# One core, a hybrid retention/RG-LRU step: raw tokens transposed first and modulated two blocks ahead, gate products moved among heads, output projection by token tiles

## The chip, the core and the metric

The kernel runs on one core of a Trainium2 chip. The metric is device time in microseconds; lower is better. Five engines work in order, each from its own queue: PE (TensorE, matmul), DVE (VectorE), ACT (ScalarE), POOL (GpSimd) and SP (SyncE, which here issues nearly all DMAs). An instruction that waits holds up everything behind it on its engine.

## The reference, cut to what matters

There are 640 tokens (512 latent, 128 context), width 1024. Both groups go through the same layer.

```
mod = silu(cond) @ w_ada + b_ada ; shift, scale, gate = split(mod, 3)
h   = rmsnorm(x, norm_w) * (1 + scale) + shift           # 640 x 1024
z   = h @ w_in     # q, k, v, g_ret, x_lru, g_lru, m_ret, m_lru
o   = retention(q, k, v), 4 heads, forward + backward    # per head normalised, * silu(g_ret)
hl  = rglru(conv(x_lru)): two sigmoid gates per direction from 10 blocks of 128x128, then a scan
merged = sigmoid(m_ret) * (o @ w_ret_down) + sigmoid(m_lru) * ((hl * silu(g_lru)) @ w_lru_down)
y   = rmsnorm(x + gate * (merged @ w_out), final_norm_w) ; also the last retention and LRU states
```

## The kernel before, in words

Every fp32 product is made from three fp32r matmuls: each operand is split into a high part (ACT copies it, `hTh`, `sh`, `yh`) and a low part (DVE subtracts, `low`, line 410: `hTl`, `sl`, `yl`). Lines 404 to 406 (`mm3`) issue the three. Weights stream through SBUF: `raw` tiles are loaded by SP in a fixed stream order, split by ACT and DVE into slabs, and used by PE. Projections run feature-major with 2 x 320 tokens, so most matmuls are 128x320; those of the heads and of the output are 128x512.

The stages, in the order of PE:

1. Start. The five token tiles `x` are normalised (`norm_x`). Then for each of 8 blocks `kt` of 128 features: `mod_mm` multiplies `c` with the block's `w_ada` (tile `adr`, eight fp32 matmuls that the trace shows as 16 rows); `mod_cols` turns the result into scale and shift columns `mA`, `mB`; `x_T` transposes the five token tiles of the block into PSUM and ACT copies them to `hf`; `h_mod` applies `mA`, `mB` on DVE, ACT writes `hTh`, DVE writes `hTl`; `z_first` multiplies the block with the first three column blocks of `w_in` (18 matmuls). `mod_mm`, the transposes and `z_first` of one block are interleaved with those of the block two ahead. PSUM tiles `b1` and `b2` hold the modulation and the transposes of all blocks. Matmuls of the identity (`warm`, line 727) keep PE busy until data are there. `token_sums` prepares four sums of token halves, for the products of stage 2 (seven products in place of eight, after Strassen and Winograd).
2. 32 pairs of column blocks of `w_in` (`Pair`), each 84 matmuls of 128x320 in three parts, `one`, `two`, `three`; a pair's weights are summed by DVE (`ta`, `tb`) and split (lines 514 to 539). Results go to DRAM. Between the pairs, and later between parts of the heads, stand the gate products of the ten LRU blocks (`gates`, 24 matmuls and eight sigmoids of 128x320, line 1126); the table `GATES_AT` says where. Behind each runs a `chain` of tanh, exp, sqrt on ACT, each with a table load, and products and scans on DVE.
3. Four heads: `v_product`, `inter`, `scores`, `kv_state`, `attend`; during the next head's `v_product` the last head's output is normalised, transposed back and gated (`y_unit`, line 1481) and stored; `y_job` loads and splits it again (`yf`, `yh`, `yl`).
4. Down projection of the retention branch (`rd`, 8 blocks of 128 output columns, each in two halves `k < 8` and `k >= 8` of 48 matmuls), then that of the LRU branch (`ld`), then the output projection (`wo`) with residual and last norm (`finish_part`, `finish_end`).

PE's order is the order of the code. The order on ACT and DVE within a stage is set when the program is built: pieces of work are generators with a priority, and a planner (`Plan`, with an assumed cost for each operation) chooses which goes next on which engine (`pump`). SP's order follows from that too.

Of the kernel before, what the change touches and what calls it, by code (L numbers as in the profile page):

```python
# [14 lines left out]
D = 1024  # L15
# [28 lines left out]
def first_col(b):  # L44
# [6 lines left out]
GATES_AT = {("A", 14): 0, ("A", 20): 1, ("A", 26): 2, (0, "kv"): 3, (1, "sc"): 4, (1, "at"): 5,  # L51
            (2, "at"): 6, (3, "at"): 7, (4, 0): 8, (4, 4): 9}


def stream_order():
    def gates(h, at):
        return [("gt", GATES_AT[h, at])] if (h, at) in GATES_AT else []

    o = [("fm", NEXT)]
    for n in range(len(PAIRS)):  # L60
        o += [("pa", n), ("pb", n)] + gates("A", n - 1)

# [205 lines left out]
class Direct:  # L268
# [20 lines left out]
P_X, P_C = 1.5, 1.5  # L289
# [3 lines left out]
def tile_hybrid_step(  # L293
# [188 lines left out]
    def split(i, raw, when, pools, keep=False):  # L482
# [6 lines left out]
        else:  # L489
            yield If(turn(i, pools, when))  # L490
            hi, lo = slab.take(pools() if reg[0] is not None else (perm,))
# [9 lines left out]
    def pair_weights(i, r0, r1, when):  # L501
# [20 lines left out]
        def part(sub, k):  # L522
            yield If(turn(i - 1, lambda: (perm, reg[0]), when, sub))
            hi, lo = slab.take((perm, reg[0]))
# [27 lines left out]
    def gate_sum(i, m, src, when):  # L552
        yield If(lambda: when if m == 0 or f"w{i - 3}" in S.named and S.named[f"w{i - 3}"].done else None)
# [160 lines left out]
    b1 = psp.tile([128, 512], F32, tag="b0", name="b")  # L714
    b2 = psp.tile([128, 512], F32, tag="b1", name="b")
# [24 lines left out]
    def mod_mm(kt):  # L740
        for k in range(8):
            g = slice(32 * (k % 4), 32 * (k % 4) + 32)
            w = ada_raw[kt][k // 2][:, 256 * (k % 2):256 * (k % 2) + 256]
            pe.matmul(out=b2[g, 0:256], lhsT=c32[:, k], rhs=w, start=(k < 4), stop=(k > 3))  # L744
        S.pe += 900.0
        for t in ada_raw.pop(kt):
            ada.give(t)
        dve0.tensor_copy(mod4[kt % 2], b2[:, 0:256])

    def mod_cols(kt):  # L750
        m = mod4[kt % 2]
        sel = pv[:, V_SEL:V_SEL + 2]
        pe.matmul(out=b2[:, 256:258], lhsT=m[:, 0:128], rhs=sel, start=True, stop=True)
        pe.matmul(out=b2[:, 258:260], lhsT=m[:, 128:256], rhs=sel, start=True, stop=True)
        S.pe += 250.0
        dve0.tensor_scalar(mB[:, kt], b2[:, 256:258], col(V_BSH, kt), None, op0=ADD)
        dve0.tensor_scalar(mA[:, kt], b2[:, 258:260], bsc1[:, kt:kt + 1], col(V_NW, kt), op0=ADD, op1=MUL)

    fulls, ready = {}, {}

    def x_T(kt):
        full = wide("hf")
        fulls[kt] = full
        for t in (4, 0, 1, 2, 3):
            o = b2[:, 384:512] if t == 4 else b1[:, 128 * t:128 * t + 128]
            pe.transpose(o, xt[t][:, 128 * kt:128 * kt + 128], ident)
        S.pe += 600.0
        act0.activation(full[:, 512:640], b2[:, 384:512], AF.Copy)
        act0.activation(full[:, 0:512], b1, AF.Copy)
# [7 lines left out]
    def h_low(kt):  # L777
        dve0.tensor_tensor(hTl[:, kt], fulls[kt], f32(hTh[:, kt]), op=SUB)
# [10 lines left out]
    def token_sums(k):  # L789
        a1, a2 = fulls[k], fulls[k + 4]  # L790
        a11, a21, a12, a22 = a1[:, 0:H], a1[:, H:NT], a2[:, 0:H], a2[:, H:NT]
        yield If(W6.room(2))
        u, w = wide("su"), wide("sw")
        s1, s2, s3, s4_ = u[:, 0:H], u[:, H:NT], w[:, 0:H], w[:, H:NT]
        yield V(H)
        dve.tensor_tensor(s1, a21, a22, op=ADD)
        yield V(H)
        dve.tensor_tensor(s2, s1, a11, op=SUB)
        yield A(NT)
        act.activation(sTh[0][:, k], u, AF.Copy)  # L800
# [12 lines left out]
        low(sTl[1][:, k], w, sTh[1][:, k])
        W6.give(w)

    def modulate(kt):
        mod_cols(kt)
        h_mod(kt)
        h_low(kt)

    for t in range(5):
        norm_x(t)
        warm(6)
    wf_high(0)
    wf_low(0)
    x_T(0)
    warm(4)
    mod_mm(0)
    load_ada(4)
    load_wf(4)  # L830
    warm(4)
    modulate(0)
    x_T(1)
    wf_high(1)
    wf_low(1)
    mod_mm(1)
    modulate(1)
    zq = [psz(), psz(), psz()]
    prep = soft()
    S.pe = 23000.0  # L840
    for e in S.clock:
        S.clock[e] = 23000.0

    def z_first(i, kt):
        S.pe = max(S.pe, ready[kt])
        fm_k([zq[i][:, 0], zq[i][:, 1]], wf_hl[kt], 128 * i, hTh[:, kt], hTl[:, kt], kt == 0, kt == 7)
        if kt > 3:
            S.pump(S.pe - 500.0)

    for kt in range(8):  # L850
        z_first(0, kt)
        if kt < 6:
            x_T(kt + 2)
            wf_high(kt + 2)
        z_first(1, kt)
        if kt < 6:
            mod_mm(kt + 2)
            wf_low(kt + 2)
        z_first(2, kt)
        if kt < 6:  # L860
            modulate(kt + 2)
# [7 lines left out]
        if kt == 3:  # L869
            job(prep, "soft", prio=4.0)  # L870
        if kt > 1 and kt < 6:
            job(token_sums(kt - 2), f"sums{kt - 2}", prio=1.5)
# [20 lines left out]
    zs = [b1, b2]  # L893
# [16 lines left out]
    for n in ["first0", "first1", "first2", "soft"] + [f"sums{k}" for k in range(4)]:  # L910
# [17 lines left out]
    tts.add(rg, [f"tt{i}" for i in range(3)])  # L928
    tmps = Slots(S)
    tmps.add(rg, ["p0", "p1"])  # L930
# [271 lines left out]
    WL.add(rg, [f"l{i}" for i in range(8)])  # L1202
    lru_jobs(("A",))
    prev = None
    for n in range(len(PAIRS) + 1):
        p = None
        if n < len(PAIRS):
            p = Pair(n)
            p.one()
        if prev:  # L1210
            prev.three()
            hook("A", n - 1)
        if p:
            p.two()
        prev = p

# [7 lines left out]
    def switch_to_heads():  # L1224
        S.until(lambda: not (W6.busy(rg) or WL.busy(rg) or tmps.busy(rg) or tts.busy(rg) or slab.busy(rg) or half.busy(rg)))
        for s in (W6, WL, tmps, tts, slab, half):
            s.drop(rg)
        reg[0] = None
        regp.__exit__(None, None, None)
        sTp.__exit__(None, None, None)  # L1230
# [50 lines left out]
    def v_product(h, between):  # L1281
        acc = {}
        for kk in range(4):
# [13 lines left out]
            between(kk)  # L1297
# [35 lines left out]
    def prompt_k(h):  # L1333
# [23 lines left out]
        job(ev(), f"kd{h}", prio=2.0)  # L1357
# [159 lines left out]
    def fetch_qk(h):  # L1517
        for s in "qk":
            for i in range(2):
                job(qk_job(s, h, i), f"{s}{h}{i}", prio=1.6)  # L1520

    for h in range(NH):
        def between(kk, h=h):
            if h == 0 and kk == 0:
                switch_to_heads()
# [417 lines left out]
```

## Time and profile before

| | |
|---|---|
| median of 3 runs | 1025.45 us (1022.33 to 1027.98) |
| the profiled execution | 1029.65 us, span from first to last instruction 1027.8 us |
| PE busy | 993.9 us (97% of the span) |
| DVE, ACT busy | 738.1 us (72%), 529.8 us (52%) |
| mean granted PE clock | 0.98 |
| DMA | 158.15 MB, mean 154 GB/s |

Busy is the time in which an engine had an instruction in work; matmuls overlap, so PE's share says only that PE rarely had none. The granted clock is the share of 2.4 GHz that PE was given; 0.50 is 1.2 GHz.

### The profile page before, as it was taken

What the parts mean: (1) busy time and instruction counts of PE and PEld (TensorE: products, weight loads), DVE (VectorE), ACT (ScalarE), POOL (GpSimd) and SP (SyncE); (2) the same over time, 40 slices, a digit from 0 to 9 for tenths busy, and PEclk for the clock granted to TensorE, in tenths of its full rate; (3) what the DMA queues carried; (4) which work ended last, traced back from release to release, by engine and by line L of the source; (5) the groups of instructions that cost most, each with busy time, mean ns of one, the idle gap of its engine ahead of it and who ended that gap; (6) DMA issues with size and microseconds to landing.
All of it is one profiled execution on the core that took longest, in us unless ns stands there. A gap on an engine that the chain in (4) does not pass through costs nothing.

```text
span 1027.8 us, 15490 instructions
## 1 busy us (share of the span) xinstructions
PE 993.9 (97%) x6057; PEld 926.3 (90%) x6057; DVE 738.1 (72%) x1148; ACT 529.8 (52%) x835; POOL 2.2 (0%) x13
## 2 busy tenths in 40 slices
PE   8987999999999999999999998999989999999996
PEld 7877999999999999999888887878869999999885
DVE  4578986777689879885576776687778974846436
ACT  5345544444675684563359277557566616424203
POOL 0000000000000000000000000000000000000000
PEclk8988999999999999999999998999999999999999
DMA  9623554443425325535433542553547655635402
GB/s 344 208 98 95 161 164 142 134 134 123 141 101 208 128 94 187 195 114 176 168 92 129 176 148 78 181 180 105 184 161 252 221 176 186 220 107 183 157 1 103
DMA packets 62168, 158.15 MB, mean 154 GB/s; under 512 B 6906, under 2 KB 10126, under 8 KB 62094
## 3 DMA queue, kind: packets, MB, share of 16 engines
q1 hardware_dynamic: 62094, 157.16, 46.4%
q8 instruction: 47, 0.77, 0.3%
q14 instruction: 27, 0.22, 0.1%
HBM read 119.51 MB, written 37.63 MB: 153 GB/s over the span
## 4 chain that ended last, share of the span: by engine, by line
PE 88%; DVE 4%; ACT 3%; DMA 3%; issue 1%; SPq 0%; ACTq 0%; DVEq 0%
PE z L404 29%; PE z L406 28%; PE z L405 28%; PE b L744 1%; DVE sl L410 1%; DMA wfr<-in_w_first_dram 1%; DMA hf<-h 1%; DMA y<-sg 1%; PE z L1481 1%; DMA yf<-y 0%; DMA x<-in_x_sample_dram 0%; ACT z L1433 0%; DVE ptl L410 0%; DVE ltl L410 0%; DVE st L1375 0%
## 5 line engine op out<-in xcount | busy, mean ns | idle before, releaser
L410 DVE TENSOR_TENSOR sl<-raw,sh 128x1024 fp32r<-128x1024 f32 (+1 forms) x128 | 133.4, 1046 | 53.5 <-ACT sh L495 52.6
L495 ACT ACTIVATE sh<-raw 128x1024 fp32r<-128x1024 f32 (+1 forms) x96 | 96.7, 1012 | 144.1 <-PE z L405 89.8
L404 PE MATMUL z<-sh,sh 128*128 128x320 f32 x512 | 159.9, 312 | 7.0 <-ACT sh L529 5.9
L406 PE MATMUL z<-sh,sl 128*128 128x320 f32 x512 | 159.8, 312 | 0.7 <-DVE sl L410 0.7
L405 PE MATMUL z<-sl,sh 128*128 128x320 f32 x512 | 159.7, 312 | 0.0
L404 PE MATMUL z<-hTh,sh 128*128 128x320 f32 x432 | 137.1, 317 | 0.0
L405 PE MATMUL z<-hTl,sh 128*128 128x320 f32 x432 | 135.1, 313 | 0.0
L406 PE MATMUL z<-hTh,sl 128*128 128x320 f32 x432 | 134.9, 312 | 0.0
L404 PEld LDWEIGHTS z<-sh,sh 128*128 128x128 f32 x512 | 97.3, 190 | 7.5 <-ACT sh L529 6.2
L406 PEld LDWEIGHTS z<-sh,sl 128*128 128x128 f32 x512 | 97.2, 190 | 1.1 <-DVE sl L410 1.1
L405 PEld LDWEIGHTS z<-sl,sh 128*128 128x128 f32 x512 | 97.3, 190 | 0.0
L404 PEld LDWEIGHTS z<-hTh,sh 128*128 128x128 f32 x432 | 82.8, 192 | 2.9 <-issue 2.5
L405 PEld LDWEIGHTS z<-hTl,sh 128*128 128x128 f32 x432 | 82.7, 191 | 0.0
L406 PEld LDWEIGHTS z<-hTh,sl 128*128 128x128 f32 x432 | 82.6, 191 | 0.0
L404 PE MATMUL z<-yh,sh 128*128 128x320 f32 x256 | 79.3, 310 | 0.0
L406 PE MATMUL z<-yh,sl 128*128 128x320 f32 x256 | 79.2, 309 | 0.0
L405 PE MATMUL z<-yl,sh 128*128 128x320 f32 x256 | 79.2, 309 | 0.0
L404 PE MATMUL z<-sh,hTh 128*128 128x512 f32 x160 | 64.3, 402 | 0.6 <-ACT gt L1126 0.6
L405 PE MATMUL z<-sl,hTh 128*128 128x512 f32 x160 | 63.5, 397 | 0.0
L406 PE MATMUL z<-sh,hTl 128*128 128x512 f32 x160 | 63.4, 396 | 0.0
L405 PE MATMUL z<-ltl,sh 128*128 128x320 f32 x160 | 49.6, 310 | 0.5 <-DVE ltl L410 0.5
L404 PE MATMUL z<-lth,sh 128*128 128x320 f32 x160 | 49.6, 310 | 0.0
(252 smaller groups left out, 2200.3 us busy)
## 6 DMA issues: line engine op xcount, KB each, us to landing
raw<-in_w_str_dram SPq DMA_DIRECT2D x131, 512.0 KB, 3.9
adr<-in_w_ada_dram SPq DMA_DIRECT2D x32, 256.0 KB, 5.2
g<-c SPq DMA_DIRECT2D x16, 320.0 KB, 2.3
sg<-g SPq DMA_DIRECT2D x16, 320.0 KB, 3.5
y<-sg SPq DMA_DIRECT2D x16, 320.0 KB, 2.6
yf<-y SPq DMA_DIRECT2D x16, 320.0 KB, 4.6
out_dram<-kv SPq DMA_DIRECT2D x16, 256.0 KB, 2.6
x<-c SPq DMA_DIRECT2D x10, 320.0 KB, 4.0
```

The source lines that it names most:

```text
L404: pe.matmul(out=out, lhsT=lh, rhs=rh, start=start, stop=False, **kw)
L405: pe.matmul(out=out, lhsT=lh, rhs=rl, start=False, stop=False, **kw)
L406: pe.matmul(out=out, lhsT=ll, rhs=rh, start=False, stop=stop, **kw)
L410: dve.tensor_tensor(out, full, f32(hi), op=SUB)
L495: act.activation(hi[:, 0:w], raw, AF.Copy)
L744: pe.matmul(out=b2[g, 0:256], lhsT=c32[:, k], rhs=w, start=(k < 4), stop=(k > 3))
L1481: pe.transpose(z[:, 128 * t:128 * t + 128] if t < 4 else zp_[:, 0:128], o[t][:, 128 * i:128 * i + 128], ident)
```

## The change

In words, in the order of the program:

- **Start.** The transposed tokens no longer wait for the modulation of their block. All eight `x_T` stand ahead of the first `z_first`, in the three large PSUM tiles `z`; blocks 1 and 3 are copied out by DVE. `mod_mm` alternates between two PSUM tiles (`mb`), `mod_mm`, `mod_cols` and `h_mod` run two blocks ahead; `h_mod` moves from DVE to ACT (Identity with scale and bias), and for blocks 0 and 1 both engines do it (ACT straight into `hTh`). There are 15 more identity matmuls ahead and 4 fewer behind. The tokens' tiles move to the other side of SBUF, so that the tiles for the pairs' weights (`ta`, `tb`, `p`) open before the first block and not behind stage 1.
- **Token sums.** Split into `sum_3` and `sum_124`, started as soon as their blocks are there, at a higher priority.
- **Gates.** Seven of ten gate products move (`GATES_AT`), four of them in heads 0 to 2, to an earlier place; the planner's costs and some priorities change.
- **Last pair.** The first quarter of head 0's `v_product` now stands ahead of the last part of the last pair.
- **Down projection.** New order of the 16 halves (`DOWN`): (0,0), (1,0), (2,0), then (0,1) and so on; head 3's four `y_unit` stand behind the first and the second of them, not ahead of all.
- **Output.** The k-outer loop over three token tiles at once is replaced by one token tile after the other.

```diff
-GATES_AT = {("A", 14): 0, ("A", 20): 1, ("A", 26): 2, (0, "kv"): 3, (1, "sc"): 4, (1, "at"): 5,
-            (2, "at"): 6, (3, "at"): 7, (4, 0): 8, (4, 4): 9}
+GATES_AT = {("A", 10): 0, ("A", 20): 1, ("A", 26): 2, (0, "sc"): 3, (1, "v3"): 4, (1, "kv"): 5,
+            (2, "sc"): 6, (3, "at"): 7, ("D", 5): 8, ("D", 9): 9}
...
+DOWN = [(0, 0), (1, 0), (2, 0), (0, 1), (1, 1), (2, 1), (3, 0), (4, 0), (3, 1), (4, 1), (5, 0), (6, 0), (5, 1), (6, 1),
+        (7, 0), (7, 1)]
...
-    def h_mod(kt):
+    def h_mod(kt, both=False):
         full = fulls[kt]
-        for c, g in ((slice(0, 512), 1), (slice(512, 640), 0)):
-            dve0.tensor_scalar(full[:, c], full[:, c], mA[:, kt, g:g + 1], mB[:, kt, g:g + 1], op0=MUL, op1=ADD)
-        act0.activation(hTh[:, kt], full, AF.Copy)
...
+            if both:
+                act0.activation(hTh[:, kt, c], full[:, c], AF.Identity, scale=a, bias=b)
...
+                act0.activation(full[:, c], full[:, c], AF.Identity, scale=a, bias=b)
+        if not both:
+            act0.activation(hTh[:, kt], full, AF.Copy)
+        dve0.tensor_tensor(hTl[:, kt], full, f32(hTh[:, kt]), op=SUB)
...
     for t in range(5):
         norm_x(t)
-        warm(6)
+        warm(9)
+    x_T(0)
+    x_T(1, dve0)
...
+    mod_mm(0, dve0)
...
+    x_T(7)
+    xtp.__exit__(None, None, None)
+    ttp, tr = open_pool("ttp", "right")
+    tts.add(tr, [f"tt{i}" for i in range(3)])
...
     for kt in range(8):
         z_first(0, kt)
+        if kt == 0:
+            mod_cols(1)
+            h_mod(1, True)
         if kt < 6:
-            x_T(kt + 2)
+            mod_mm(kt + 2)
             wf_high(kt + 2)
         z_first(1, kt)
         if kt < 6:
-            mod_mm(kt + 2)
+            mod_cols(kt + 2)
             wf_low(kt + 2)
+            h_mod(kt + 2)
         z_first(2, kt)
-        if kt < 6:
-            modulate(kt + 2)
...
+        if n == len(PAIRS):
+            next(v_first)
         if prev:
             prev.three()
...
+    for n, (m, half_k) in enumerate(DOWN):
+        if n in (1, 2):
+            for i in (2 * n - 2, 2 * n - 1):
+                y_unit(NH - 1, i)
+        if n == 2:
+            switch_to_down()
...
+    for t, c0, n, i in parts:
...
+        accs = [bank()] if t else [bank(), bank()]
+        for k in range(8):
+            if t == 0:
+                wo[k] = take(("wo", k))
+                need(f"ml{k}")
+            for b, a in enumerate(accs):
+                out_mm(a[:, 0:n], c0 + 512 * b, n, t, k)
```

Three places of the instruction order. First PE at the start, where the identity matmuls ahead of the first transposes end; before:

```order
L766 MATMUL b<-ident,x_110 128x128
L727 MATMUL z<-ident 128x128 x4
L744 MATMUL b<-adr,c_114 32x256 x8
L727 MATMUL z<-ident 128x128 x4
L753 MATMUL b<-pv,mod_112 128x2
L754 MATMUL b<-pv,mod_112 128x2
L766 MATMUL b<-ident,x_111 128x128
```

The same place now (L781 is `x_T`, L754 `mod_mm`, L766 and L767 `mod_cols`):

```order
L781 MATMUL z<-ident,x_111 128x128
L736 MATMUL b<-ident 128x128 x2
L754 MATMUL b<-adr,c_117 32x256 x8
L781 MATMUL z<-ident,x_107 128x128
L781 MATMUL z<-ident,x_108 128x128
L781 MATMUL z<-ident,x_109 128x128
L781 MATMUL z<-ident,x_110 128x128
L781 MATMUL z<-ident,x_111 128x128
L736 MATMUL b<-ident 128x128 x2
L766 MATMUL b<-pv,mod_115 128x2
L767 MATMUL b<-pv,mod_115 128x2
L781 MATMUL z<-ident,x_107 128x128
```

Block 2's transposes stand between block 0's modulation matmuls and its columns, and more transposes follow directly; before, the columns stood between two stretches of identity matmuls.

Second, ACT at the passage from the start to the first pair. Before (`m<-z`, `m<-b` are the first sigmoids, `sw`, `su` the token sums, `p<-z` the copy of pair 0's first product, `tb`, `ta` pair 0's summed weights):

```order
L886 ACTIVATE m<-z 128x640
L904 ACTIVATE m<-b 128x320 x2
L811 ACTIVATE sh_101<-sw 128x640
L800 ACTIVATE sh_100<-su 128x640
L811 ACTIVATE sh_101<-sw 128x640
L707 ACT_TABLE_LOAD
L707 ACTIVATE qdec<-qdec 128x32
L708 ACTIVATE kdec<-kdec 128x8
L952 ACTIVATE p<-z 128x320
L539 ACTIVATE sh<-raw 128x512
L495 ACTIVATE sh<-raw 128x1024
L539 ACTIVATE sh<-raw 128x512
```

Behind these follow, before, the splits of `tb` and `ta` (L529). Now:

```order
L944 ACTIVATE m<-z 128x640 x2
L848 ACTIVATE sh_100<-s_765 128x640
L944 ACTIVATE m<-z 128x640
L848 ACTIVATE sh_100<-s_803 128x640
L539 ACTIVATE sh<-tb 128x1024
L962 ACTIVATE m<-b 128x320 x2
L539 ACTIVATE sh<-ta 128x1024
L858 ACTIVATE sh_101<-s_764 128x2x320
L1007 ACTIVATE p<-z 128x320
```

The split of `tb` has moved ahead of `m<-b`, that of `ta` directly behind it, and the table load with `qdec`, `kdec` to a later place.

Third, ACT in head 1, where the gates' sigmoids stood at the end of the head (L1126 `gt`; L1433 squares of the head's output, L1440 its norm, L1158 the chain's square root, L1413 `kv`):

```order
L1158 ACTIVATE th<-th 128x640
L1427 ACTIVATE o<-z 128x512
L1433 ACTIVATE z,ssq<-o 128x512 x2
L1440 ACTIVATE rst<-ssq,epsc 128x5
L1158 ACTIVATE th<-th 128x640
L1126 ACT_TABLE_LOAD
L1126 ACTIVATE gt<-z,pv 128x320 x4
L1413 ACTIVATE kv<-z 128x512 x2
```

In head 1 now, the first of the two gate products stands behind the last quarter of `v_product` (L1317 splits `v`, L1181 is `gt`, L1361 the start of `inter`):

```order
L1317 ACTIVATE vh<-z 128x512 x5
L505 ACTIVATE sh<-raw 128x1024
L1181 ACT_TABLE_LOAD
L1181 ACTIVATE gt<-z,pv 128x320 x4
L505 ACTIVATE sh<-raw 128x512
L1181 ACTIVATE gt<-z,pv 128x320 x2
L1361 ACTIVATE o<-z,qdec 128x512
L1181 ACTIVATE gt<-z,pv 128x320 x2
```

The second gate product of head 1 moved from behind `attend` to between `kv_state` and `attend`.

## Rows read from the trace of the kernel before

**Rows 1.** The page: span and PE's line.
```profile
span 1027.8 us, 15490 instructions
...
PE 993.9 (97%) x6057; PEld 926.3 (90%) x6057; DVE 738.1 (72%) x1148; ACT 529.8 (52%) x835; POOL 2.2 (0%) x13
```

**Rows 2.** PE's waits over the span: total us, times, longest.
```profile
PE z L404 <- ACT sh L529: 5.9, 1, 5.9
PE b L744 <- ACT hf L284: 5.7, 3, 4.3
PE z L404 <- ACT gt L1126: 2.7, 2, 2.1
PE z L404 <- ACT pph L1378: 2.1, 1, 2.1
PE z L1481 <- ACT gt L1126: 1.5, 1, 1.5
```

**Rows 3.** Windows: length, busy us by engine, PE clock, DMA share, GB/s.
```profile
28.00:32.84 4.84, 4.84 (x48) 4.06 (x44) 2.93 (x7) 1.80 (x4) 0.00 (x0) 1.00 1.00 326
49.90:55.80 5.90, 1.58 (x13) 1.32 (x10) 4.61 (x10) 2.52 (x5) 0.00 (x0) 0.85 0.25 86
55.80:64.00 8.20, 8.18 (x40) 6.91 (x41) 3.59 (x8) 2.55 (x4) 0.00 (x0) 0.50 0.22 65
77.90:84.20 6.30, 0.36 (x3) 0.16 (x1) 5.31 (x17) 5.92 (x10) 0.00 (x0) 0.77 0.07 11
84.20:91.60 7.40, 6.65 (x24) 6.25 (x25) 7.33 (x10) 2.23 (x3) 0.00 (x0) 0.50 0.52 144
100.00:150.00 50.00, 50.00 (x343) 50.00 (x342) 43.29 (x62) 26.40 (x40) 0.00 (x0) 1.00 0.49 154
```

**Rows 4.** Timeline of PE: start, us, line, operation; first transposes, block 0, pair 1.
```profile
12.79 0.77 PE L766 MATMUL b<-ident,x 128*128 128x128 f32 x5 [0.38 <-DVE x L284]
13.40 1.06 PE L727 MATMUL z<-ident 128*128 128x128 f32 x8
14.71 1.07 PE L744 MATMUL b<-adr,c 128*32 128x256 f32 x16 [0.26 <-ACT hf L284]
...
22.66 0.61 PE L404 MATMUL z<-hTh,sh 128*128 128x320 f32 x1
...
93.41 0.31 PE L404 MATMUL z<-hTh,sh 128*128 128x320 f32 x1
```

**Rows 5.** Groups by shape in 0 to 60 us: count, busy us, mean ns, idle before.
```profile
L284 ACT ACTIVATE hTh<-hf 128x640 fp32r<-128x640 f32 x7 | 5.2, 738 | 23.6 <-DVE hf L284 23.6
...
L284 DVE TENSOR_TENSOR hTl<-hf,hTh 128x640 fp32r<-128x640 f32 x7 | 5.8, 825 | 5.6 <-ACT hTh L284 5.6
```

**Rows 6.** Windows in heads 1 and 3 and behind.
```profile
564.00:592.00 28.00, 28.00 (x134) 22.91 (x133) 20.93 (x33) 7.29 (x11) 0.00 (x0) 1.00 0.51 171
599.00:625.00 26.00, 23.49 (x117) 19.82 (x115) 17.64 (x28) 22.68 (x40) 0.00 (x0) 0.98 0.47 146
625.00:631.00 6.00, 5.19 (x17) 4.81 (x18) 4.54 (x7) 4.83 (x11) 0.00 (x0) 0.51 0.23 87
746.00:750.00 4.00, 1.91 (x9) 1.16 (x7) 4.00 (x8) 2.14 (x5) 0.00 (x0) 1.00 0.79 252
750.00:754.00 4.00, 4.00 (x12) 2.98 (x11) 3.74 (x6) 2.26 (x5) 0.00 (x0) 0.57 0.94 346
```

**Rows 7.** Timelines of SP and DVE at the start of the down projection.
```profile
774.81 1.86 SPq L591 DMA_DIRECT2D y<-sg  x2
776.72 3.79 SPq L596 DMA_DIRECT2D yf<-y  x8
...
790.17 0.82 DVE L410 TENSOR_TENSOR yl<-yf,yh 128x640 fp32r<-128x640 f32 x1
```

**Rows 8.** Timeline of the end: last matmul, last stores.
```profile
1019.31 0.28 PE L406 MATMUL z<-sh,ml 128*128 128x256 f32 x1
...
1023.08 1.94 SPq L1779 DMA_DIRECT2D out_dram<-u  x4
```

More of the change, by code (lines that the diff above doesn't have):

```diff
@@ L490, in split @@
             yield If(turn(i, pools, when))
-            hi, lo = slab.take(pools() if reg[0] is not None else (perm,))
+            hi, lo = slab.take([p for p in pools() if p is not None])
         grant(i)
@@ L523, in part @@
             yield If(turn(i - 1, lambda: (perm, reg[0]), when, sub))
-            hi, lo = slab.take((perm, reg[0]))
+            hi, lo = slab.take([p for p in (perm, reg[0]) if p is not None])
             grant(i - 1, sub)
@@ L759, in tile_hybrid_step, with x_T @@
+        pe.matmul(out=b[:, 258:260], lhsT=m[:, 128:256], rhs=sel, start=True, stop=True)
+        S.pe += 300.0
+        dve0.tensor_scalar(mB[:, kt], b[:, 256:258], col(V_BSH, kt), None, op0=ADD)
+        dve0.tensor_scalar(mA[:, kt], b[:, 258:260], bsc1[:, kt:kt + 1], col(V_NW, kt), op0=ADD, op1=MUL)
     fulls, ready = {}, {}
-    def x_T(kt):
+    groups = ((slice(0, 512), 1), (slice(512, 640), 0))
+    def x_T(kt, eng=act0):
         full = wide("hf")
         fulls[kt] = full
-        for t in (4, 0, 1, 2, 3):
-            o = b2[:, 384:512] if t == 4 else b1[:, 128 * t:128 * t + 128]
+        z = psz()
+        for t in range(5):
+            o = z[:, 1, 0:128] if t == 4 else z[:, 0, 128 * t:128 * t + 128]
@@ L1200, in hook @@
             gates(j)
[L1202 to L1215, printed above, removed]
     hdp = [None]
@@ L1224, in switch_to_heads @@
     def switch_to_heads():
-        S.until(lambda: not (W6.busy(rg) or WL.busy(rg) or tmps.busy(rg) or tts.busy(rg) or slab.busy(rg) or half.busy(rg)))
-        for s in (W6, WL, tmps, tts, slab, half):
+        S.until(lambda: not (W6.busy(rg) or WL.busy(rg) or tmps.busy(tr) or tts.busy(tr) or slab.busy(rg) or half.busy(rg)))
+        for s in (W6, WL, slab, half):
             s.drop(rg)
@@ L1279, in v_job, with v_product @@
         banks.give(ps)
-    def v_product(h, between):
+    def v_product(h):
         acc = {}
@@ L1519, in fetch_qk @@
             for i in range(2):
-                job(qk_job(s, h, i), f"{s}{h}{i}", prio=1.6)
-    for h in range(NH):
-        def between(kk, h=h):
-            if h == 0 and kk == 0:
-                switch_to_heads()
-                job(strip_job(0), "strip0", prio=3.0)
-                lru_jobs(range(5))
+                job(qk_job(s, h, i), f"{s}{h}{i}", prio=1.4)
+    WL.add(rg, [f"l{i}" for i in range(8)])
+    lru_jobs(("A",))
+    prev, v_first = None, v_product(0)
+    for n in range(len(PAIRS) + 1):
+        p = None
+        if n < len(PAIRS):
+            p = Pair(n)
+            p.one()
+        if n == len(PAIRS):
+            next(v_first)
+        if prev:
+            prev.three()
+            hook("A", n - 1)
+        if p:
+            p.two()
+        prev = p
+    switch_to_heads()
+    job(strip_job(0), "strip0", prio=3.0)
+    lru_jobs((0, 1, 2, 3, "D"))
+    fetch_qk(0)
+    for h in range(NH):
+        for kk in v_first if h == 0 else v_product(h):
             if h and kk:
                 y_unit(h - 1, kk - 1)
-            if h == 0 and kk == 0:
-                fetch_qk(0)
             hook(h, f"v{kk}")
-        v_product(h, between)
         if h:
@@ L1552, in tile_hybrid_step @@
         hook(h, "at")
-    for i in range(4):
-        y_unit(NH - 1, i)
-        S.pump()
-    hd = hdp[0][1]
-    S.until(lambda: not (W6.busy(hd) or W5.busy(hd)))
-    W6.drop(hd)
-    W5.drop(hd)
-    hdp[0][0].__exit__(None, None, None)
-    regC = ctx.enter_context(tc.tile_pool(name="regC", bufs=1, reuse_waits="tile"))
-    W6.add(regC, [f"c{i}" for i in range(38)])
-    for i in range(8, 16):
-        job(y_job(i // 4, i % 4, W6), f"y_{i}", prio=1.0)
     sig, ro = {}, {}
@@ L1715, in tile_hybrid_step @@
         W6.give(lt[k][1])
-    S.until(lambda: all(S.named[f"w{i}"].done for i in range(len(order)) if order[i][0] == "ga" and f"w{i}" in S.named))
+    need("ga7")
     load_rows(0, gbias)
```

286 lines of the change are left out of this document (157 added, 129 removed).

## The prediction

> **What bounds the kernel now.** I read the page first, then PE's waits, then windows over the stretches in which PE's share is low, then the timelines there. PE has something in work for 97% of the span [rows 1], so PE's order is the path that sets the end, and 33.9 us without PE work are all that its waits can hold. But a busy PE is not always a fast PE: in four stretches the granted clock is 0.50 or little more, that is 1.2 GHz [rows 3, 6], and each of them follows a wait. A steady stretch shows the full rate: 343 matmuls of 128x320 in 50 us, 0.146 us each, at clock 1.00 [rows 3].
>
> Two of the waits stand in the passage from the start to the first pair: the modulation matmuls of block 7 wait 4.3 us for ACT to empty the PSUM tile with block 7's transposes, and pair 0's second product waits 5.9 us for its split weights [rows 2]. After each, PE runs at 1.2 GHz, for 8.2 us (55.8 to 64.0) and 7.4 us (84.2 to 91.6) [rows 3]. The rest stands in the heads: 2.1 us for `gt` at the end of head 1, 2.1 us for `pph` in head 3, 1.5 us for `gt` ahead of head 3's `y_unit` [rows 2]; the first two are again followed by clock 0.51 and 0.57 over 6 and 4 us [rows 6].
>
> **The change, term by term. The front.** Before, block 0's first product starts at 22.66 and pair 1 at 93.41 [rows 4]; I count how long the new order takes to the same two points.
>
> To block 0: the identity matmuls now run 15 longer, 30 rows in the trace. Eight rows take 1.06 us [rows 4], 0.13 each; so they end some 3 to 4 us after the 12.79 at which transposes began before, near 16. Behind them PE has eight sets of transposes (0.55 to 0.77 us, upper end as in [rows 4]), two `mod_mm` at about 1.0 (1.07 there), four identity matmuls and one `mod_cols`, together about 1.0: 7.4 to 9.2 us, so 23.4 to 25.2. ACT and DVE copy out meanwhile; block 0's `hTl` needs five PSUM copies, `hTh` and DVE's own 0.83 [rows 5] behind the tokens, and comes at about 24 too. I take 24.0: a loss of 1.3 against 22.66.
>
> From there each block costs what block 28.00 to 32.84 costs, 4.84 us [rows 3], less one set of transposes (0.55 to 0.77) and a wait of some 0.1 to 0.2: 4.1. It can be no less, since 18 matmuls at 0.146 are 2.6 and the modulation takes 1.5. Can ACT keep that? Per block it has the copy of `mod`, the weights' high part, two parts of `h_mod` and `hTh` 0.74 [rows 5], under 3.3 us with a token sum, and the results are needed a block later; so PE sets the period. Six blocks of 4.1 and two of 2.6 give 29.8, the column block behind them 48 x 0.146 = 7.0, pair 0's first two products 24 x 0.146 = 3.5, its next three 36 x 0.146 = 5.3. Sum from 24.0: pair 1 at 69.6, with some 0.9 for small waits 70.5, against 93.41: **-23**.
>
> Nothing may wait then at the passage. Before, the tiles of `tb` and `ta` opened only behind stage 1, and the token sums stood ahead of them. Now the tiles are free at the start, and in ACT's order the split of `tb` stands ahead of `m<-b`. From block 7's `hTl` at about 51, DVE has about 13 us of work up to `sl<-tb`, ready at about 64 against the 64.8 at which PE wants it. That is tight: what DVE loses there, PE waits. The bounds of this term are -25 (no small waits) and -13 (the wait of 5.9 stays, with its slow stretch, in which 24 matmuls do the work of 3.5 us in 6.7).
>
> A rule bears on the clock. The Trainium skill, "TensorE: Matmul & The Clock Gate", section "HAM oscillation — how this bites in real kernels", says that waits between groups of matmuls make the clock fall and that each restart is paid anew. The trace agrees: waits of 4.3 and 5.9 us are followed by 0.50 [rows 2, 3], while the 1.5 us for `gt` cost no clock. By that rule the new front, whose waits are under 1 us, stays at 2.4 GHz; if it did not, the third rival below would hold.
>
> **The heads.** At 599 to 625 ACT is busy 22.7 of 26 us, at 564 to 592 only 7.3 of 28 [rows 6]: head 1 has two gate products behind its scores, whose 16 sigmoids, tanh, exp, sqrt and table loads all fall into the same stretch. Moving the first into `v_product` puts some 11 us of ACT work (an estimate: eight sigmoids, six passes over 640 columns, three table loads) into the slack. What is left for ACT from the scores to the norm I sum to about 21 us against 24 us of PE work. So the 3.3 us without PE work (2.5 of the 26 and 0.8 of the 6) go, and the 6 us at 0.51 lose about 2.7 us less: **-6**. Against it: DVE has 20.9 of 28 busy there already [rows 6] and gets about 10 us of the first chain, where 7.1 are free; I set **+1** for waits on late `v`, `o` and `st`, bounds 0 and +4. The wait of 1.0 at the last pair is covered by 30 matmuls of 128x512 that now stand ahead (about 6.8 us), and the shorter waits for `gt` and `hl` parts behind moved gates go as well: **-2** together, bounds 0 and -3.
>
> Head 3's wait for `pph` I leave: ACT stands behind `yh`, which waits for loads of `y`, and SP's order there is nearly the same as before; now three `yh` instead of two stand between the first and the second score tile. **0**, bounds -3.7 (2.1 and the clock) and +1.
>
> **Down projection.** The 1.5 us for `gt` is covered by the first half (0,0), 48 x 0.146 = 7.0 us. But head 3's last two `y_unit` now stand behind it and (1,0), and only (2,0), 7 us, lies between them and (0,1), which needs all of heads 2 and 3. Before, the last `yl` came at 791.0, 14.3 us after the first of the eight loads at 776.7, and 14 us of matmuls lay between [rows 7]. Now the loads can be issued some 2.6 us behind the last `y_unit`, and `yl` 8 is wanted 13.2 us behind it: 2.6 + 14.3 - 13.2 = 3.7 us late, less what DVE is spared of gate 7's chain and of gate sums. I take 2: **+0.5** net, bounds -1.5 and +2.2.
>
> **The end.** The output projection has the same matmuls. Its first tile now takes a slab of `w_out` every 1.3 us instead of 3.9, but the last operand `ml7` is wanted 9 us behind the LRU projection and takes about 6. Before, the finish of token tile 3 ran into that of tile 4: behind the last matmul (1019.31 + 0.28) four stores were issued, the last at 1025.0 [rows 8]. Now DVE and ACT have one tile there, and the last of two stores goes out some 1.7 us earlier: **-1.7**, bounds -0.5 and -2.5.
>
> **Sum.** -23 - 6 + 1 - 2 + 0 + 0.5 - 1.7 = -31.2. The profiled execution took 1029.65, so 998.5 for such a one; it stands 4.2 above the median of the runs shown (1025.45), and in medians the sum gives 994.3. I say **995 us**.
>
> **The rivals.** *Head work returns.* The front gains, but the heads' waits only change their place: DVE in head 1 is the new bound (+4), the down projection waits its 3.7, and nothing else is won. -23 - 1.7 + 4 + 2.2 - 2 = -20.5, so 1005. For it speaks DVE's 20.9 of 28 [rows 6]; against it that ACT, not DVE, was full where PE waited.
>
> *Pair 0's weights stay late.* The wait in front of the second product stays: -13 for -23 in the front, so 1005 again, or 1010 together with half of the first rival. For it speaks the margin of under 1 us; against it that DVE is not held by anything but its own order.
>
> *Slower: the front stays cold.* If the granted clock stood at 0.50 from the first transposes on, as at 55.8 to 64.0, a matmul of 128x320 would take 0.27 and not 0.146 (24 in 6.65 us at 84.2 to 91.6 [rows 3]), 1.85 times as long. The 54 us from 16 to 70 would cost 46 more: 995 + 46 = 1041. It decides from 37 us of such work on (31.2 / 0.85). Against it: from 28 us on the old kernel runs at 1.00 with the same mix [rows 3], and the new one has PE fuller.
>
> *No effect.* PE has work 97% of the time already [rows 1], so nothing is to be had but what waits hold; if the freed stretches were taken up by other waits, 1025. The Trainium skill, "Perfetto Trace Analysis", section "Identifying the Most-Contended Engine", calls PE's busy share a bad measure of what is left. The trace agrees: 40 rows took 8.2 us at 55.8 to 64.0 and count as 8.18 busy [rows 3].
>
> **Chances.** Forecast 0.58 (its own range 986 to 1001); head work returns 0.20 (1001 to 1010); late weights 0.13 (1002 to 1014); no effect 0.05; slower 0.04. 984 comes about if head 3's wait and the down projection's go too; I leave out 2 in 10, mostly above, and give 985 to 1010. A measurement of this kernel can tell about 0.5%, 5 us, from no change: faster 0.91, within 0.5% 0.05, slower 0.04.
>
> **What would show it.** Right: first product of block 0 near 24 us; blocks every 4.1 us; pair 1 near 70; no clock under 0.9 between 20 and 90; no wait for `tb` or `ta`; ACT fuller in head 1's `v_product` and no wait for `gt` at its end; a wait of some 2 us for `yl` at (0,1); two stores behind the last matmul. The forecast is wrong if pair 1 starts behind 78, or if the waits from 480 us on sum to as much as before.

## The result, and the profile after

The changed kernel takes 998.67 us (median of 4 runs, 998.22 to 999.64) against 1026.49 us before (4 runs on the same chip, 1022.33 to 1027.98): ratio 0.9737, 95% interval 0.9706 to 0.9768. The profiled execution took 999.01 us against 1029.65. The forecast was 995 (985 to 1010): the sign and the main places were right, and four steps were mis-sized or wrong.

The page after: span, busy time of the engines; to be read beside [rows 1].
```profile
span 997.2 us, 15542 instructions
...
PE 981.6 (98%) x6079; PEld 918.0 (92%) x6079; DVE 732.3 (73%) x1133; ACT 543.6 (55%) x856; POOL 2.2 (0%) x13
```
PE is busy 12 us less while the span is 31 us shorter: 18 us of waits went, and 12 us of busy time, for the most part matmuls at 1.2 GHz. PE's waits after, total, times, longest, beside [rows 2] (L414 to L416 are `mm3` now, L420 is `low`, L294 a helper through which ACT and DVE get their work at the start):
```profile
PE z L414 <- ACT pph L1419: 2.9, 1, 2.9
PE z L414 <- ACT gt L1181: 1.5, 1, 1.5
...
PE z L414 <- ACT hTh L294: 1.1, 1, 1.1
PE z L415 <- DVE yl L420: 1.0, 1, 1.0
```
PE's timeline after, to be read beside [rows 4]: the first transposes, block 0, pair 1.
```profile
15.18 1.25 PE L781 MATMUL z<-ident,x 128*128 128x128 f32 x10
...
23.11 0.41 PE L414 MATMUL z<-hTh,sh 128*128 128x320 f32 x1
...
73.92 0.31 PE L414 MATMUL z<-hTh,sh 128*128 128x320 f32 x1
```
The waits of 5.9 for `sh`, 4.3 for `hf` and 2.1 for `gt` are gone; the one for `pph` has stayed and grown.

To see where the time came from I took the first product of each stage from PE's timeline in both traces. Between pair 1 and the LRU projection the two kernels do the same PE work (head 3's four `y_unit` are in both), so the differences add up to that of the spans:

| stretch of PE's order | before, us | after, us | difference | forecast |
|---|---|---|---|---|
| start to pair 1 | 93.41 | 73.92 | -19.5 | -23 |
| pair 1 to head 1's first product | 461.63 | 459.50 | -2.1 | -2, with the rest of the heads |
| head 1 | 74.14 | 69.12 | -5.0 | -6 + 1 |
| head 2 | 68.00 | 65.10 | -2.9 | (in the -2) |
| head 3 and down projection | 193.52 | 195.20 | +1.7 | 0 + 0.5 |
| LRU and output projections | 128.89 | 128.12 | -0.8 | 0 |
| end of the last matmul to end of span | 8.25 | 6.28 | -2.0 | -1.7 |
| sum | 1027.8 | 997.2 | -30.6 | -31.2 |

Windows after (length, busy us by engine, PE clock, DMA share, GB/s): a block of the front, the stretch ahead of block 7's first product, head 1's `v_product`, head 1 from its scores on, and head 3 around its scores.
```profile
28.60:32.90 4.30, 4.30 (x40) 3.52 (x39) 2.67 (x7) 3.37 (x7) 0.00 (x0) 1.00 1.02 371
49.10:53.95 4.85, 3.73 (x26) 3.48 (x26) 3.17 (x12) 1.99 (x4) 0.00 (x0) 1.00 0.14 23
542.00:570.00 28.00, 28.00 (x141) 23.52 (x141) 22.18 (x34) 15.93 (x24) 0.00 (x0) 1.00 0.51 172
577.00:603.00 26.00, 25.95 (x124) 21.69 (x123) 23.90 (x37) 22.67 (x41) 0.00 (x0) 1.00 0.50 160
715.00:720.00 5.00, 2.80 (x13) 1.97 (x11) 5.00 (x10) 3.93 (x8) 0.00 (x0) 1.00 0.77 267
720.00:725.00 5.00, 4.35 (x13) 3.54 (x14) 4.89 (x9) 4.56 (x10) 0.00 (x0) 0.71 0.36 137
```
A block takes 4.30 us (4.84 in [rows 3]). Head 1's `v_product` has 15.9 us of ACT work where [rows 6] had 7.3; ACT is as full from the scores on as it was, but PE no longer waits there. Head 3's wait for `pph` is still followed by a low clock. The kernel before had a fifth slow stretch, which the prediction does not name: from 20 to 27 us, around its block 0, the mean clock was 0.52. It is gone too.

### The profile page after: what moved, and what is told of

Its sections match the earlier page's. It is cut to its first block, busy times and chain, and to the rows that moved or that the text cites. A ratio compares the mean times of both kernels' runs of the same rounds, so it can differ in the third digit from the quotient of the medians.

```text
span 997.2 us, 15542 instructions
## 1 busy us (share of the span) xinstructions
PE 981.6 (98%) x6079; PEld 918.0 (92%) x6079; DVE 732.3 (73%) x1133; ACT 543.6 (55%) x856; POOL 2.2 (0%) x13
## 4 chain that ended last, share of the span: by engine, by line
PE 91%; DVE 4%; ACT 3%; issue 1%; DMA 1%; POOL 0%; DVEq 0%; POOLq 0%; ACTq 0%
PE z L414 29%; PE z L415 29%; PE z L416 29%; PE b L736 1%; PE z L1522 1%; ACT hf L294 1%; DVE sl L420 1%; ACT hTh L294 1%; DVE hTl L294 1%; DMA y<-sg 0%; DMA yf<-y 0%; ACT sh L539 0%; PE z L781 0%; ACT gt L1181 0%; DVE st L1416 0%
## 5 line engine op out<-in xcount | busy, mean ns | idle before, releaser
L420 DVE TENSOR_TENSOR sl<-raw,sh 128x1024 fp32r<-128x1024 f32 (+1 forms) x128 | 133.2, 1045 | 50.2 <-ACT sh L505 49.8
L414 PE MATMUL z<-sh,sh 128*128 128x320 f32 x512 | 158.5, 310 | 0.7 <-ACT p L1007 0.7
L416 PE MATMUL z<-sh,sl 128*128 128x320 f32 x512 | 158.4, 309 | 0.0
L414 PE MATMUL z<-hTh,sh 128*128 128x320 f32 x432 | 134.6, 311 | 1.1 <-ACT hTh L294 1.1
L416 PE MATMUL z<-hTh,sl 128*128 128x320 f32 x432 | 133.2, 308 | 0.0
L414 PEld LDWEIGHTS z<-sh,sh 128*128 128x128 f32 x512 | 96.1, 188 | 1.3 <-ACT p L1007 1.3
L416 PEld LDWEIGHTS z<-sh,sl 128*128 128x128 f32 x512 | 96.1, 188 | 0.0
L414 PEld LDWEIGHTS z<-hTh,sh 128*128 128x128 f32 x432 | 81.1, 188 | 3.9 <-issue 2.5
L416 PEld LDWEIGHTS z<-hTh,sl 128*128 128x128 f32 x432 | 81.1, 188 | 0.0
L414 PE MATMUL z<-yh,sh 128*128 128x320 f32 x256 | 79.4, 310 | 1.6 <-ACT gt L1181 1.5
L416 PE MATMUL z<-yh,sl 128*128 128x320 f32 x256 | 79.0, 309 | 0.0
L414 PE MATMUL z<-sh,hTh 128*128 128x512 f32 x160 | 63.7, 398 | 0.0
L416 PE MATMUL z<-sh,hTl 128*128 128x512 f32 x160 | 63.2, 395 | 0.0
L1054 ACT ACTIVATE p<-z 128x320 f32<-128x320 f32 x32 | 14.0, 437 | 67.3 <-PE z L416 67.3
L414 PEld LDWEIGHTS z<-yh,sh 128*128 128x128 f32 x256 | 48.1, 188 | 2.2 <-ACT gt L1181 1.7
```

What stands on the lines that cost most here:

```text
L414: pe.matmul(out=out, lhsT=lh, rhs=rh, start=start, stop=False, **kw)
L416: pe.matmul(out=out, lhsT=ll, rhs=rh, start=False, stop=stop, **kw)
L420: dve.tensor_tensor(out, full, f32(hi), op=SUB)
L1054: act.activation(self.tmp[:, 2], self.a[:, 0:H], AF.Copy)
```

## The experiments

Each is an edit of the changed kernel, except the first. In all of them the computation is unchanged. They were measured on several chips, each beside the kernel before, whose medians there lay between 1025.7 and 1026.9 us. The changed kernel was not measured again, so a difference of 1 or 2 us from its 998.67 is weak by itself; the stages of the profiled executions are read with it.

**1. The front alone.** The kernel before, with the new start, block loop, token sums and place of the tiles for `ta` and `tb`, and nothing else of the change.

> The kernel before with the new front alone (start, block loop, token sums, place of the tiles for ta and tb); gates, heads, down projection and output stay as before. Theory: the terms add up, so this kernel starts pair 1 near 73.9 us, as the changed one does, and takes 19.5 us less than before, 1007 us, with head 1's wait for gt (2.1 us, clock near 0.5 behind it) still there. Rival: the front's gain leans on what was changed behind it, or the later stages take part of it back by waits for loads and splits that now come earlier: pair 1 near 74 all the same, but a time of 1012 us or more.

Measured: 1009.97 us against 1026.02, ratio 0.9842 (0.9811 to 0.9873). Pair 1 starts at 74.40, with a mean clock below 1 behind block 7, which the changed kernel's profile does not have; head 1 waits 1.2 and 2.1 us as before, and head 3 and the down projection take 193.8 us as before. The profiled execution took 1010.13, 19.5 less than the profiled one of before, as the theory has it; the medians differ by 16.0 only. The time lies between the theory's 1007 and the rival's 1012. In profiled executions the terms add up, and the mark that I set was wrong in the same way as the forecast: it took the difference of two profiled executions off a median (below).

**2. Gates back.**
```diff
-GATES_AT = {("A", 10): 0, ... (0, "sc"): 3, (1, "v3"): 4, (1, "kv"): 5, (2, "sc"): 6,
+GATES_AT = {("A", 14): 0, ... (0, "kv"): 3, (1, "sc"): 4, (1, "at"): 5, (2, "at"): 6,
```


> The changed kernel with gate products 0 to 6 at their old places (7, 8 and 9 stay at the new ones). Theory: the places of the gates are what shortened heads 1 and 2 by 5.0 and 2.9 us, since ACT was full behind head 1's scores: the time comes back to 1006 or 1007 us, with a wait of some 2 us for gt at the end of head 1 and a granted clock near 0.5 behind it. Rival: most of it came from the changed priorities (splits of q and k, kd, the gate chains) and the early first slab of head 0: then the time is 1002 us or less and head 1 has no wait over 1 us for gt.

Measured: 1004.89 us, ratio 0.9797 (0.9769 to 0.9825), 6.2 above the changed kernel's median. PE's waits for `gt` in this run, of which 2.7 us stand at the end of head 1 and 1.5 ahead of half (0,0):
```profile
PE z L414 <- ACT gt L1181: 4.2, 2, 2.7
```
Heads 1 and 2 take 72.13 and 65.67 us in place of 69.12 and 65.10. The time stays under the theory's 1006, and the clock behind the wait was 1.00 and not near 0.5. So the places of the gates are worth 5 to 6 of the 8 us that I gave them: 6.2 by the medians, and by the stages of the profiled execution 3.0 in head 1, 1.5 in the pairs and 0.6 in head 2. The other 2.3 us of head 2's gain come from elsewhere in the change. In the kernel before, head 2 has waits of 0.6 us for `kdh` and 0.6 for a slab of weights, which are gone, and the end of the slow stretch behind head 1; which edit took them away, no run here shows.

**3. Old order of the down projection**, with head 3's `y_unit` ahead.
```diff
-DOWN = [(0, 0), (1, 0), (2, 0), (0, 1), (1, 1), (2, 1), (3, 0), (4, 0), (3, 1), (4, 1), ...
+DOWN = [(0, 0), (1, 0), (0, 1), (1, 1), (2, 0), (3, 0), (2, 1), (3, 1), (4, 0), (5, 0), ...
-        if n in (1, 2):
-            for i in (2 * n - 2, 2 * n - 1):
+        if n == 0:
+            for i in range(4):
```


> The changed kernel with the down projection's halves in the old order and head 3's four y_unit ahead of them. Theory: the new order covered nothing, since half (0,0) itself waits for the PSUM banks that gate 7's sigmoids hold; undone, the wait for gt (1.5 us) moves to the first y_unit, the wait for yl (1.0 us) goes, and head 3 with the down projection takes 194 us in place of 195.2; whole time 997.5 us. Rival, as I forecast: the new order saves the 1.5 us, so undone it costs them and saves 1.0: 999.2 us or more.

Measured: 1001.58 us, ratio 0.977 (0.9743 to 0.9797). The wait of 1.5 for `gt` moved to the first `y_unit` and that for `yl` fell to 0.3, as the theory says. But two waits of 1.1 us came up that neither theory has: the gates behind the sixth and tenth half now find four PSUM banks held by half-done products. Head 3 and the down projection take 199.3 us, 5 more than forecast; the rival's time came (999.2 or more), but not by its cause. So the run does not price the order alone; it shows that the new order saved nothing on the `gt` wait, and that these two gates cost 1.1 us each where products are open and nothing in the changed kernel, where none is.

**4. Old output loop.** `finish` and the output loop as before the change.

> The changed kernel with the output projection's old loop (three token tiles at once over k, then tiles 3 and 4). Theory: the new loop gains behind the last matmul alone, 8.5 us before against 6.5 now; undone, four stores go out behind the last matmul and the time is 2.0 us higher, 1000.7 us, with the same 57.3 us from the first product to the last. Rival: the tail is set by tile 4 alone, so it stays at 6.5 us and the time within 0.5 us of 998.7.

Measured: 1000.50 us, ratio 0.9757 (0.9732 to 0.9782). The 57.6 us from the first output product to the end of the last matmul are the same; behind it stand 8.2 us in place of 6.3. The new loop is worth 2 us, all in the tail.

**5. Block 7 ahead of the sums.**
```diff
-        S.pump(S.pe)
+        if (kt, i) not in ((4, 2), (5, 0), (5, 1)):
+            S.pump(S.pe)
```


> The changed kernel with DVE's token sums of the last two blocks of the modulation put behind block 7's mB, mA and hTl instead of ahead of them; soft's eight short operations stay. Theory: the 1.1 us for hTh and 0.4 for hTl before block 7's first product are there because four sums and splits (2.2 us) stand ahead of mB in DVE's queue; without them block 7 starts 1.5 to 2 us earlier, pair 1 about 49.3 us behind block 0's first product in place of 50.8 to 51.7, and the time is 997.0 us. Rival: DVE is the bound of this stretch, since from 48 to 68 us it is idle for only 1.6 us; then the same time is lost a little later, at pair 0's S2 or S1 products, and pair 1 stays 50.5 us or more behind block 0.

Measured: 998.03 us, ratio 0.9735 (0.9696 to 0.9773). PE's waits from 20 to 80 us, of this run:
```profile
PE z L414 <- ACT p L1008: 1.5, 1, 1.5
PE z L415 <- DVE hTl L294: 0.5, 2, 0.3
```
The wait for `hTh` is gone and has come back 15 us later: pair 1 stands 50.78 us behind block 0's first product, 50.81 in the changed kernel. The rival holds: with block 7 ahead in DVE's queue, something else is late.

**6. Also `soft` later.** `soft`'s short operations run behind pair 2.

> As the run with block 7 ahead, and soft's operations (2.3 us of DVE between 49 and 66 us) moved behind pair 2. If DVE is the bound of the stretch, taking 2.3 us of its work out gains up to as much: pair 1 about 48.8 us behind block 0 and 996.5 us. If the order alone was at fault, this run is like the one before it, within 0.3 us in the front.

Measured: 997.97 us, ratio 0.9737 (0.9688 to 0.9787), pair 1 50.4 us behind block 0: 0.4 us for 1.6 us of DVE work less (the expectation says 2.3; `soft`'s eight operations sum to 1.6 in the trace). What is last there is a chain over both engines: `p`'s copy (the wait is 1.8 us now) stands on ACT behind the last sums' `sh`, which waits for DVE.

**7. Loads of `y` later.**
```diff
     def y_job(h, i, slots):
+        if h < 2 and 4 * h + i > 1:
+            yield after(f"st{NH - 1}3")
```


> The changed kernel with six of the eight loads and splits of y in head 3 held back until its fourth score tile is split. Theory: the 2.9 us for pph come from the yh that wait for their loads in ACT's queue ahead of the score tiles' splits (one of them 2.5 us); without them the wait goes, and with it the stretch at clock 0.71: head 3 up to the down projection 4 us shorter, 994.5 us. Rival: the score tiles are late because of DVE (strip product, splits, and 5 us of conv) or the splits of y now stand in front of attend's evictions: the wait only moves, and the time stays above 997.5 us.

Measured: 993.60 us, ratio 0.969 (0.9652 to 0.9728). Windows of this run around head 3's scores:
```profile
715.00:720.00 5.00, 5.00 (x24) 3.66 (x23) 5.00 (x10) 3.02 (x7) 0.00 (x0) 1.00 1.00 372
720.00:725.00 5.00, 5.00 (x24) 4.13 (x23) 4.67 (x9) 2.68 (x5) 0.00 (x0) 1.00 0.92 312
```
No wait for `pph`, none for `gt`, and 24 rows in each 5 us at clock 1.00, where the changed kernel had 13, during the wait and then at 0.71. Gate 7's sigmoids start at 732.1 here, ahead of the norm's square root at 738.6, so half (0,0) finds its PSUM banks free. The cause stands in ACT's queue of the changed kernel, where a split of `y` waits for its load while the score tiles stand behind it:
```profile
711.60 0.74 ACT L1553 ACTIVATE yh<-yf 128x640 fp32r<-128x640 f32 x1 [2.54 <-DMA yf<-y]
```

**8. Gate 7 moved** from behind head 3's attend to its `v_product` (`(3, "at"): 7` to `(3, "v3"): 7`).

> The changed kernel with gate 7 moved from behind head 3's attend to the end of its v_product. Theory: the 1.5 us that half (0,0) waits are for PSUM banks that gate 7's sigmoids hold, which stand behind the norm's sqrt and two table loads in ACT's queue; with no gate there the wait goes: 1.5 us less there. ACT has 11 us more work ahead of the scores, which pushes yh back; if that takes yh out of the way the pph wait goes too and the time is 993 us. Rival: the gate's sigmoids and chain make the score tiles' splits later, the pph wait grows by 2 us or more, and the time is 999 us or more.

Measured: 995.57 us, ratio 0.9711 (0.9673 to 0.9749). The `gt` wait is gone and `pph`'s is 0.5: the gate's sigmoids, ahead of the splits of `y` in ACT's order, pushed these out of the scores. Between the two marks, since `yl` is now late three times, 1.9 us in all, and in the profiled execution the front takes 0.9 us longer, at a lower clock behind block 7.

**9. Token sums on GpSimd**, on top of run 6: `dve.tensor_tensor` becomes `pool.tensor_tensor` in four lines, which are 16 operations in the trace (the expectation says 14), each 0.48 us on DVE.

> As the run with block 7 ahead and soft later, and the 14 additions of the token sums put on GpSimd in place of DVE, which takes about 6 us of DVE's work out of the stretch from 32 to 68 us. If DVE's whole work is what bounds the passage to pair 0, pair 1 comes 49.3 us or less behind block 0, 1.1 us less than with soft later alone, and the wait for p falls under 0.5 us. Rival: GpSimd takes longer for an addition than DVE's 0.48 us, or slows DVE beside it, and the sums come later than now: pair 1 stays 50.4 us or more behind block 0 and the wait for p grows.

Measured: 997.65 us, ratio 0.971 (0.9697 to 0.9723). Pair 1 stands 48.93 us behind block 0, 1.5 less than in run 6, and the wait for `p` is 0.6. So DVE's work was the bound, for 1.9 us (50.81 to 48.93): taking some 9 us of it out of the stretch gained no more. The price can be seen on GpSimd's timeline of this run, and in the second block on DVE's:
```profile
38.28 0.87 POOL L844 TENSOR_TENSOR s<-hf 128x320 f32<-128x320 f32 x1 [3.42 <-ACT hf L294]
...
56.60 6.20 POOL L844 TENSOR_TENSOR s<-hf 128x320 f32<-128x320 f32 x1 [5.12 <-DVE sl L420]
62.88 1.21 POOL L845 TENSOR_TENSOR s<-s,hf 128x320 f32<-128x320 f32 x1
```
```profile
58.91 0.68 DVE L530 TENSOR_TENSOR ta<-raw 128x512 f32<-128x512 f32 x1
...
63.38 1.25 DVE L528 TENSOR_TENSOR tb<-raw,tb 128x512 f32<-128x512 f32 x1
```

**10. Together:** runs 6 and 7, and the four `y_unit` all behind half (0,0).

> Block 7 ahead, soft later and the loads of y later in one kernel, and head 3's four y_unit all between the halves (0,0) and (1,0), 7 us earlier for the last two. By the sum of the runs before: 5 us for the loads of y and 0.4 for the front from 998.7, and if the last y_unit's place sets yl, its wait of 1.0 us goes: 992.3 us. If y_unit now waits itself, for the norm or for PSUM banks, as much is lost there as the wait for yl was: 993.3 us.

Measured: 993.47 us, ratio 0.9669 (0.9656 to 0.9682). The wait for `yl` falls to 0.2, and a `y_unit` waits 1.2 us instead, for PSUM banks that DVE's `sg` product holds. Nothing is won by its place.

**11. Fewer identity matmuls** (`warm(9)` back to `warm(6)`).

> The changed kernel with 15 identity matmuls less at the start, 6 behind each token tile as before the change. Theory: they only fill PE while it waits for the tokens; block 0's first product stays within 0.6 us of 23.1, since ACT's and DVE's work on the tokens sets it, the granted clock behind it is 1.00, and the time stays within 1 us of 998.7. Rival 1: they stand on the path, and block 0 comes 1 us earlier or more. Rival 2: they hold the clock up, and without them the transposes or block 0 run at 0.5 and the time is 2 us higher or more.

Measured: 996.67 us, ratio 0.9704 (0.9686 to 0.9721). The theory falls, rival 1 holds. The start of this run on PE's timeline:
```profile
12.88 0.88 PE L781 MATMUL z<-ident,x 128*128 128x128 f32 x6 [0.83 <-DVE x L294]
...
20.44 0.41 PE L414 MATMUL z<-hTh,sh 128*128 128x320 f32 x1
```
PE now waits for the last token tile, so the tokens are ready at 12.9; in the changed kernel the transposes begin at 15.18, behind the last identity matmul, and block 0 at 23.11. The 15 matmuls cost 2.7 us by these two profiles, and the median is 2.0 lower; over all profiles block 0 came between 22.57 and 23.98 with them, at 20.44 and 20.73 without (runs 11 and 12). The clock is 1.00 without them too, from 5 to 50 us.

**12. All that was found:** runs 7, 9 (with 5 and 6) and 11 in one kernel.

> What the runs so far found, in one kernel: 15 identity matmuls less at the start, block 7 ahead, soft later, token sums on GpSimd, loads of y in head 3 later; the y_unit stay where the changed kernel has them. If the terms add up (2.7 us at block 0, 1.9 us up to pair 1, 5.0 us in head 3), the front ends near 69.5 us and the time is 989 us. Rival: the blocks now start before their operands, so part of the 2.7 us turns into waits for loads or for DVE's and ACT's results in the block loop, and the time is 991 us or more.

Measured: 989.50 us (5 runs, 989.09 to 990.40), ratio 0.9637 (0.9615 to 0.9659): 9.2 us below the changed kernel. Pair 1 starts at 69.66, and 24 or 25 rows run in each 5 us of head 3's scores. The three terms add up within the scatter of each: 998.67 - 2.7 - 1.9 - 5.0 = 989.1.

## Why the prediction was right, and where it was wrong

**The step from sum to median was wrong, and is most of the miss.** The sum was -31.2 and -30.6 came: 998.5 forecast for a profiled execution, 999.01 measured. That the sum is so close is in part luck: the front fell 3.5 us short and head 3 with the down projection 1.2, while the pairs and head 2 gave 3.0 more than forecast, the LRU and output projections 0.8 and the end 0.3. Then I took 4.2 us off, because the profiled execution of before stood that much above its median. That distance belongs to the kernel before alone. Its runs in all comparisons here, 1021.8 to 1029.7, go with their mean granted clock: 0.990 in those near 1022, 0.980 to 0.983 in those above 1028.7. The changed kernel has hardly a low stretch left in its profile, and its four runs lie within 1.4 us. Not all the spread went with the low stretches, though: the runs of experiments 6 and 11 lie within 4.0 us each, and 11's again by clock (0.998 in its fastest, 0.994 in its slowest).

**Front: -19.5 for -23, mechanism right.** Pair 1 came at 73.92 for 70.5; there is no low clock from 20 to 90 in this profile and no wait for `ta` or `tb`. Block 0 came at 23.11, 0.9 better than the term; but of what I took as its cost, the identity matmuls alone are 2.7 (run 11). From block 0 to pair 1 it took 50.8 us for the 45.6 of the sum (46.5 with small waits). Of these 5.2 us the first block has 1.3 (5.44 for 4.1), the next five, alike at 4.30, have 1.0, blocks 6 and 7 have 2.2 (3.91 and 3.46 for 2.6 each), and pair 0's first products 0.6. So the cost of a block on PE was set too low, without any wait behind the first. The step that failed is "so PE sets the period". It held up to block 6, not for block 7, whose columns came late from DVE. DVE's timeline ahead of it:
```profile
48.31 0.82 DVE L294 TENSOR_TENSOR hTl<-hf,hTh 128x640 fp32r<-128x640 f32 x1 [1.88 <-ACT hTh L294]
49.05 0.17 DVE L294 TENSOR_SCALAR small<-small 128x28 f32<-128x28 f32 x1
...
50.35 0.82 DVE L420 TENSOR_TENSOR sl<-s,sh 128x640 fp32r<-128x640 f32 x1
51.09 0.48 DVE L844 TENSOR_TENSOR s<-hf 128x320 f32<-128x320 f32 x1
51.49 0.21 DVE L294 TENSOR_SCALAR mB<-b,pv 128x2 f32<-128x2 f32 x1
51.62 0.27 DVE L294 TENSOR_SCALAR mA<-b,bsc,pv 128x2 f32<-128x2 f32 x1
```
Between `hTl` of block 6 and `mB` of block 7, which PE had ready at 49.2, stand 2.4 us of `soft` and token sums. I had counted ACT's work per block, and DVE's only up to `sl<-tb`. The margin that I called tight was at the right place: by runs 5 and 9 DVE's work up to pair 0 costs 1.9 us. Run 12's pair 1 at 69.66 looks like the 69.6 of the sum, but by luck: its block 0 came at 20.73, not 24.0, and the way from there took 48.9 us, not 45.6.

**Head 1: -5.0 for -6 + 1.** Right in place and cause (run 2). Of it 3.3 us are the two waits before. The 1 us that I added for a fuller DVE did not come: it had 22.2 of 28 us and held nothing up.

**Small waits: -2 was too small**; the pairs gave -2.1 and head 2 alone -2.9. My bound of 3 rested on the waits alone. The stretch at clock 0.51 in [rows 6] goes to 631, and head 2 began at 629.2; that part of the low clock I had booked to head 1.

**Head 3 and down projection: +1.7 for +0.5.** `pph` was rightly left uncovered, and cost 0.8 more. The wait for `yl` came where forecast, 1.0 for 2. These two make up the +1.7. Wrong is "the 1.5 us for `gt` is covered by the first half (0,0)": that half itself needs two PSUM banks, and these are held until ACT has done gate 7's sigmoids, which stand behind the norm:
```profile
735.63 1.28 ACT L1481 ACT_TABLE_LOAD   x1
736.92 0.30 ACT L1481 ACTIVATE rst<-ssq,epsc 128x5 f32<-128x5 f32 x1
737.24 1.28 ACT L1181 ACT_TABLE_LOAD   x1
738.54 0.95 ACT L1181 ACTIVATE gt<-z,pv 128x320 f32<-128x320 f32 x2
```
I had looked for what the half reads and not for where it writes.

**End: -2.0 for -1.7.** Two stores behind the last matmul (990.68 + 0.28), the last issued 3.9 us behind its start; 5.7 us in [rows 8]:
```profile
993.78 0.81 SPq L1836 DMA_DIRECT2D out_dram<-u  x2
```

**The rivals.** Head work did not come back, pair 0's weights were not late, and the front was not cold in the changed kernel's profile. In five of eight profiles with the same waits ahead of block 7 it was, for a few us behind that block (last section); that sign of the prediction came true in part by luck.

## What to carry to other kernels

Before you say that PE will not wait, sum the work of each engine that feeds it up to the passage, and look in its queue for what stands ahead of the small operation on which all depends; taking an instruction ahead in a full queue only moves the wait (run 5), taking work off the queue shortens it (run 9). A product needs free PSUM banks as much as operands, and a load that comes late blocks, by the split that waits for it, all that stands behind on the same engine (run 7). When you turn a sum made from one profiled execution into a median, ask whether the spread comes from something that the change removes.

## What the runs showed of the hardware that I had not expected

The same wait does not always have the same price in clock. Windows of run 3 and of the changed kernel, both behind waits of 1.1 us for `hTh` and 0.4 for `hTl` of block 7:
```profile
55.00:60.00 5.00, 5.00 (x25) 5.00 (x25) 4.96 (x8) 4.51 (x6) 0.00 (x0) 0.66 0.37 106
```
```profile
55.00:60.00 5.00, 5.00 (x35) 5.00 (x35) 5.00 (x8) 4.34 (x6) 0.00 (x0) 1.00 0.38 116
```
25 rows in the one and 35 in the other; over all profiles with these two waits, three kept the clock and five lost it. The wait for `pph` shows it too: it was 2.7 us in runs 5 and 9, and the 5 us that follow had 22 rows at clock 1.00 in run 5 and 15 at 0.66 in run 9. In run 2 a wait of 2.7 us for `gt` was followed by clock 1.00; before the change two of 1.2 and 2.1 us, close together, went with 0.51. The Trainium skill, "TensorE: Matmul & The Clock Gate", section "HAM oscillation — how this bites in real kernels", lets each long gap be paid anew; the kernel before agrees for 4.3 and 5.9 us, and these runs show that between 1 and 3 us it goes either way. What decides, they don't show.

GpSimd and DVE hold each other up. An addition of 128x320 takes 0.87 us on GpSimd alone (0.48 on DVE); in run 9 one took 6.2 us while eight DVE operations ran one behind the other, and DVE's subtractions of 128x512 took 1.25 us beside GpSimd's in place of 0.68. (Spans on GpSimd are rough in these profiles.) The Trainium skill, "SBUF — State Buffer", section "Who interferes with whom", says that a DVE instruction with two SBUF inputs contends with a GpSimd one that reads SBUF, and calls the lock on the port pair they share exclusive. The trace agrees that each holds the other up; that one GpSimd instruction can be held up over eight of DVE, the 6.2 us show.
